# A hybrid attention, RWKV-7 and expert-retrieval layer: block-diagonal solves, a float16 choice of experts, and 24 gathered rows beside the gates

## The chip, the cores and the metric

The kernel runs on one core of a Trainium2 chip. A core has TensorE (PE: matrix products; PEld are its weight loads), VectorE (DVE), ScalarE (ACT), GpSimd (POOL) and SyncE (SP), which work side by side, and 16 DMA engines. The metric is the time of one execution on the device in microseconds (us), as the median of several runs. Times inside the execution come from one profiled execution.

## The reference

One layer over 512 latent tokens and 256 context tokens, width 1024, float32. The first half projects the normalized tokens to three branches: differential attention (8 heads), RWKV-7 heads that run in both directions (16 heads), and gates that merge the two. The recurrence of one RWKV head is

```
sa = S kk ;  S = S * w - sa (kk * a)^T + v k^T ;  y = S r
```

once in the order of the tokens and once against it. The second half is a retrieval of single-neuron experts (PEER). For every token and each of 8 heads, the 16 best of 128 row keys and the 16 best of 128 column keys are taken, then the 16 best of the 16 x 16 sums:

```
top_s, pos = lax.top_k(cand, PEER_TOPK)
eidx = jnp.take_along_axis(cidx, pos, axis=-1)
gate = jax.nn.softmax(top_s, axis=-1)
act = jax.nn.gelu(einsum('chkd,cd->chk', peer_u[eidx], xc))
out = einsum('chk,chkd->cd', gate * act, peer_v[eidx])
```

## The kernel before

The code states the work in a program order. A planner in the compiler fixes the order of every engine's instructions when the kernel is built: it simulates the program, and takes on each engine the earliest piece of work in program order that its simulation holds ready and for which a buffer is free. On the chip every engine then works through its list in that order and waits, instruction by instruction, for semaphores. A tile name in a pool has a number of buffers (bufs); a new tile of the name waits until one of them is released.

The stages, in order:

- *rw_pairs* (some 60 to 560 us): projections of the RWKV heads, eight pairs of heads. For each pair, *rw_scores* computes products of 32 tokens (a chunk), in two directions, and stores them: tD (what the triangular inverse needs), cbD and KBD. *rw_inverse* inverts the 32x32 triangles on VectorE and stores them as xD.
- The projections of the attention (560 to 740 us).
- *rwkv_chain* with the attention interleaved (742 to 1056 us for the chain). It takes 24 chunks of 32 tokens in sequence, each in two groups g of 4 pairs. Per group and chunk: *reads* (16 products against the state), a copy by ScalarE into rhs, *solve* (products with the inverted triangles XTz; here 16 of 128x32 weights by 64 columns, for two halves j and two directions), copies of the result into sv (the state's operand, 32 of its 128 rows) by ScalarE for one half and by VectorE for the other, *state* (16 products), a scaling by VectorE into the next sv, and *outputs* and *collect*. A float32 product shows as two records. The operands cb and KBt of the next chunk are loaded by SP, those of XTz and of the values (rows of sv) by POOL, each into one of two or three buffers. The unused parts of XTz and the 32 rows of sv that solve fills are zeroed by POOL once.
- The last heads of the attention, the merge of the branches and the output projection (to 1270 us).
- *peer_route* (1282 to 1558 us): the queries, and the choice of experts with top16 on VectorE for 8 heads and 4 blocks of 128 tokens. At its end the 16 chosen positions of each head are turned into keys: for each of 4 token blocks and each of the two keys (8 turns), VectorE compares 128 positions with 16 numbers (L995), multiplies with the keys (L999), and sums over the 16 (L1000).
- *peer_gates* (to 1749 us). For 384 of the tokens the experts are not gathered: all 16,384 experts are computed as dense blocks of 128, and a gate matrix picks the chosen ones. It is built in 12 chunks of 32 tokens from float16 compares and multiplies (tiles oa, obh, obl, two buffers each; L1045 to L1048), products (L1053, L1054), copies into the one stage buffer and a store of 2 MB to gD.
- *block_acts*: the product of a block of 128 experts' in-weights with the 384 tokens (ps_a; the weights split into a high and a low part by ScalarE, u_hi, L69, and VectorE, u_lo, L72). 72 of the 128 blocks come before 1757 us, as filler in routing and gates, and are parked in actD.
- The first output loop (1760 to 2243 us): for the other 56 blocks the in-product, gating, the split of the out-weights (v_hi L1132, v_lo L1133) and 18 products into ps_v per block.
- The last output loop (2243 to 2578 us): the 72 parked blocks, 18 products each, with loads of the out-weights, of the gates (gg) and of the parked activations (actl) for 8 blocks at a time.

The last 128 tokens go another way, *rows*: 128 steps gather one row of peer_u for each token by an indirect DMA of POOL (a tile gr of 128x1024 float32, 5 buffers) and take its dot product with the token (L1087), then 128 steps gather a row of peer_v and add it to the result ra (L1098). The call some(n) takes n steps of these. They start when the pool gr is opened, after the gates: 3 steps per block of the first output loop, then 2, 1, 1 in turn.

The PSUM banks: the scores of the attention (atp) have 2 buffers, its outputs 1 and, for the last 7 blocks, 3 (atr); the chain takes the rest.

## Time and profile before

| | |
|---|---|
| runs before | median 2586.62 us of 3 (2585.44 to 2592.0) |
| the profiled execution | 2591.84 us, with a span of 2590.1 us |
| busy over the span | PE 2411.5 us (93%), DVE 2025.8 (78%), ACT 1184.6 (46%), POOL 482.8 (19%) |
| mean granted TensorE clock | 0.976 of full speed |
| HBM | 470.93 MB read, 105.38 MB written, 223 GB/s over the span |
| chain that ended last | PE 62%, DVE 20%, DMA 9%, ACT 4%, issue 4% |

Busy shares are means over stages with different limits. A busy PE is not PE at its peak, since pipelined products overlap; the idle time of an engine, and what released it, says more. "Landing" of a DMA is the time from its issue to its last byte.

### The profile page before, as it was taken

What the parts mean: (1) busy time and instruction counts of PE and PEld (TensorE: products, weight loads), DVE (VectorE), ACT (ScalarE), POOL (GpSimd) and SP (SyncE); (2) the same over time, 40 slices, a digit from 0 to 9 for tenths busy, and PEclk for the clock granted to TensorE, in tenths of its full rate; (3) what the DMA queues carried; (4) which work ended last, traced back from release to release, by engine and by line L of the source; (5) the groups of instructions that cost most, each with busy time, mean ns of one, the idle gap of its engine ahead of it and who ended that gap; (6) DMA issues with size and microseconds to landing.
All of it is one profiled execution on the core that took longest, in us unless ns stands there. A gap on an engine that the chain in (4) does not pass through costs nothing.

```text
span 2590.1 us, 46535 instructions
## 1 busy us (share of the span) xinstructions
PE 2411.5 (93%) x18109; PEld 2078.5 (80%) x18109; DVE 2025.8 (78%) x3919; ACT 1184.6 (46%) x2171; POOL 482.8 (19%) x518
## 2 busy tenths in 40 slices
PE   6999999899979999899899989998999999988898
PEld 3778778798967878668688979997888998866777
DVE  5779998977748767774499998775778888788894
ACT  4666666633336666652344444552333333323332
POOL 0000000000043333000000000013444444444430
PEclk8999999999989999999899999999999999999999
DMA  5367756787487766235432536779899999899983
GB/s 226 95 164 197 185 149 167 185 264 246 136 210 209 186 175 180 81 102 166 131 109 85 176 130 232 268 284 366 313 336 336 340 339 339 324 363 372 358 327 101
DMA packets 310349, 579.75 MB, mean 224 GB/s; under 512 B 83761, under 2 KB 197041, under 8 KB 303345
## 3 DMA queue, kind: packets, MB, share of 16 engines
q1 hardware_dynamic: 253040, 387.09, 46.6%
q0 software_dynamic: 45808, 155.61, 17.5%
q10 hardware_dynamic: 11280, 34.08, 4.1%
q8 instruction: 142, 2.33, 0.4%
q14 instruction: 79, 0.64, 0.1%
HBM read 470.93 MB, written 105.38 MB: 223 GB/s over the span
## 4 chain that ended last, share of the span: by engine, by line
PE 62%; DVE 20%; DMA 9%; ACT 4%; issue 4%; SPq 0%; POOL 0%; ACTq 0%; DVEq 0%; POOLq 0%
PE ps_v L1143 6%; PE ps_v L1145 6%; PE ps_v L1142 6%; PE ps_a L80 5%; PE ps_a L78 5%; PE ps_a L79 5%; PE pp L79 3%; PE pp L80 3%; PE pp L78 3%; PE ps_s L675 2%; PE ps_br L79 2%; PE ps_br L80 2%; PE ps_br L78 2%; DMA cb<-cbD 2%; PE ps_o L808 2%
## 5 line engine op out<-in xcount | busy, mean ns | idle before, releaser
L78 PE MATMUL ps_a<-h,u_hi 128*128 128x384 f32 x1024 | 346.2, 338 | 10.0 <-ACT u_hi L69 10.0
L80 PE MATMUL ps_a<-h,u_lo 128*128 128x384 f32 x1024 | 347.2, 339 | 7.0 <-DVE u_lo L72 6.7
L79 PE MATMUL ps_a<-h,u_hi 128*128 128x384 f32 x1024 | 344.2, 336 | 0.0
L1080 POOL DMA_INDIRECT gr<-in_peer_u,ei x128 | 165.4, 1292 | 693.1 <-PE ps_a L79 472.5
L69 ACT CAST u_hi<-u_raw 128x1024 fp32r<-128x1024 f32 x128 | 134.3, 1051 | 289.8 <-PE ps_a L79 274.1
L72 DVE TENSOR_TENSOR u_lo<-u_raw,u_hi 128x1024 fp32r<-128x1024 f32 x128 | 156.3, 1221 | 102.4 <-ACT u_hi L69 101.1
L1080 POOL DMA_INDIRECT gr<-in_peer_v,ei x128 | 179.8, 1405 | 203.7 <-DVE ra L1098 182.6
L78 PEld LDWEIGHTS ps_a<-h,u_hi 128*128 128x128 f32 x1024 | 192.8, 188 | 16.1 <-ACT u_hi L69 13.7
L80 PEld LDWEIGHTS ps_a<-h,u_lo 128*128 128x128 f32 x1024 | 192.7, 188 | 12.7 <-DVE u_lo L72 11.6
L79 PEld LDWEIGHTS ps_a<-h,u_hi 128*128 128x128 f32 x1024 | 192.7, 188 | 2.4
L1098 DVE SCALAR_TENSOR_TENSOR ra<-gr,wk,ra 128x1024 f32<-128x1024 f32 x127 | 162.7, 1281 | 2.6 <-DMA gr<-in_peer_v,ei 1.5
L95 ACT CAST w_hi<-w_raw 128x1024 fp32r<-128x1024 f32 (+1 forms) x93 | 106.9, 1149 | 125.1 <-PE ps_br L79 59.3
L96 DVE TENSOR_TENSOR w_lo<-w_raw,w_hi 128x1024 fp32r<-128x1024 f32 (+1 forms) x93 | 125.0, 1344 | 49.5 <-ACT w_hi L95 43.8
L1087 DVE CUSTOM_DVE_ANT_0 gr<-gr,ht 128x1024 f32<-128x1024 f32 x128 | 153.8, 1219 | 11.2 <-DMA gr<-in_peer_u,ei 11.2
L1143 PE MATMUL ps_v<-v_lo,pw_hi 128*128 128x512 f32 x420 | 145.0, 403 | 12.0 <-DVE v_lo L1133 12.0
L1142 PE MATMUL ps_v<-v_hi,pw_hi 128*128 128x512 f32 x420 | 128.5, 400 | 16.0 <-ACT v_hi L1132 16.0
L546 PE MATMUL pp<-At,kz 128*128 128x128 f32 x768 | 106.2, 295 | 35.7 <-DVE kz L539 15.4
L78 PE MATMUL pp<-hx,w_hi 128*128 128x512 f32 x336 | 134.9, 402 | 3.4 <-ACT sgw L433 2.4
L80 PE MATMUL pp<-hx,w_lo 128*128 128x512 f32 x336 | 134.1, 399 | 2.0 <-DVE w_lo L96 2.0
L79 PE MATMUL pp<-hx,w_hi 128*128 128x512 f32 x336 | 133.0, 396 | 1.8 <-DVE hx L231 1.8
L1145 PE MATMUL ps_v<-v_hi,pw_lo 128*128 128x512 f32 x420 | 134.1, 401 | 0.0
L546 PEld LDWEIGHTS pp<-At,kz 128*128 128x128 f32 x768 | 98.4, 207 | 42.9 <-ACT kt L550 18.5
(374 smaller groups left out, 6390.7 us busy)
## 6 DMA issues: line engine op xcount, KB each, us to landing
u_raw<-in_uT SPq DMA_DIRECT2D x128, 512.0 KB, 4.6
v_raw<-in_peer_v SPq DMA_DIRECT2D x70, 512.0 KB, 8.3
w_raw<-in_peer_v SPq DMA_DIRECT2D x58, 512.0 KB, 6.5
wm<-in_w_mod SPq DMA_DIRECT2D x24, 1024.0 KB, 8.8
cb<-cbD SPq DMA_DIRECT2D x48, 512.0 KB, 6.5
gD<-gstage SPq DMA_DIRECT2D x12, 2048.0 KB, 8.3
gg<-gD SPq DMA_DIRECT2D x16, 1536.0 KB, 13.4
actD<-act SPq DMA_DIRECT2D x18, 768.0 KB, 3.6
```

The lines of the kernel that those rows point to most:

```text
L69: nc.scalar.copy(hi, raw)
L72: (lo_eng or nc.vector).tensor_tensor(lo, raw, hi.bitcast(F32), op=OP.subtract)
L78: mm(ps, lh[0], rh[0], start=first, stop=False)
L79: mm(ps, lh[0], rh[1], start=False, stop=False)
L80: mm(ps, lh[1], rh[0], start=False, stop=last)
L546: nc.tensor.matmul(ps[:, c, :], kz[:, c, :], at, start=True, stop=True)
L1080: nc.gpsimd.indirect_dma_start(out=r, out_offset=None, in_=self.A[name], in_offset=bass.IndirectOffsetOnAxis(ap=self.ei[:, k:k + 1], axis=0))
L1087: nc.vector.tensor_tensor_reduce(out=r, in0=r, in1=self.ht, scale=1.0, scalar=0.0, op0=OP.mult, op1=OP.add, accum_out=w[:, k:k + 1])
L1098: nc.vector.scalar_tensor_tensor(self.ra, r, w[:, k:k + 1], self.ra, op0=OP.mult, op1=OP.add)
L1142: mm(pc[t][d], w[0][:, ts], v[0][:, c[d]], start=first, stop=False)
L1143: mm(pc[t][d], w[0][:, ts], v[1][:, c[d]], start=False, stop=False)
L1145: mm(pc[t][d], w[1][:, ts], v[0][:, c[d]], start=False, stop=last)
```

## The change

- *Solve.* The triangles of the two halves and two directions of a pair are laid out as one 128x128 block-diagonal matrix (XTz as [128, 8, 4, 32]), so that one product of 128-column weights takes the place of four of 32-column weights. The direction 1 uses the other 32 rows of each half, so rw_scores, the mask and the zeroing swap places accordingly; tD is stored per direction (96 stores, before 48), a solve's result is one PSUM tile, and its four parts are copied to sv by two copies of ScalarE and two of VectorE, each half as large. The loads of XTz write runs of 32 elements.
- *Choice of experts.* The compare, the multiply and the sum run on float16 pairs: three halving adds and a closing add take the place of the reduction; the keys are copied to float16 pairs by ScalarE.
- *24 rows beside the gates.* After each of the 12 gate chunks two steps of rows are taken. Their tiles share the name and the two buffers of obl. The last loop takes one step per block.
- *PSUM.* The scores get 3 buffers, the last attention blocks 2.

```diff
             for j in range(2):
-                q2 = slice(64 * j + 32, 64 * j + 64)
-                nc.sync.dma_start(tD[j, cc].rearrange("c a d s t -> s (c a d) t"),
-                                  tt[q2].rearrange("p c d t -> p (c d) t"))
+                for dr in range(2):
+                    q = slice(64 * j + 32 - 32 * dr, 64 * j + 64 - 32 * dr)
+                    nc.sync.dma_start(tD[j, cc, :, dr].rearrange("c a s t -> s (c a) t"), tt[q, :, dr])
...
-        clear = lambda j, i: nc.gpsimd.memset(sv[j][i][96 - 64 * j:128 - 64 * j], 0.0)
+        vrow = lambda j, d: slice(64 - 64 * j + 32 * d, 96 - 64 * j + 32 * d)
+        urow = lambda j, d: slice(96 - 64 * j - 32 * d, 128 - 64 * j - 32 * d)
+        clear = lambda j, i: [nc.gpsimd.memset(sv[j][i][urow(j, d), d], 0.0) for d in range(2)]
         NL = 2
-        XTz = [mk(f"XTz{i}", [128, 4, 8, 32]) for i in range(NL)]
+        XTz = [mk(f"XTz{i}", [128, 8, 4, 32]) for i in range(NL)]
...
-                nc.gpsimd.dma_start(XTz[c % NL][32 * q:32 * q + 32, q], self.xD[q // 2, c, q % 2])
+                nc.gpsimd.dma_start(XTz[c % NL][32 * q:32 * q + 32, :, 3 - q], self.xD[q // 2, c, q % 2])
...
-            pu = [self.psc.tile([128, 2, 4, 64], F32, name=f"ps_u{j}") for j in range(2)]
-            for dp in range(8):
-                for j in range(2):
-                    q, ur = 2 * j + dp % 2, 96 - 64 * j
-                    nc.tensor.matmul(pu[j][ur:ur + 32, dp % 2, dp // 2, :], XTz[c % NL][:, q, 4 * g + dp // 2, :],
-                                     rhs[g][:, dp // 2, :], start=True, stop=True)
+            pu = self.psc.tile([128, 4, 64], F32, name="ps_u")
+            for a in range(4):
+                nc.tensor.matmul(pu[:, a, :], XTz[c % NL][:, 4 * g + a].rearrange("p u t -> p (u t)"), rhs[g][:, a, :],
+                                 start=True, stop=True)
             G = slice(4 * g, 4 * g + 4)
-            nc.scalar.copy(sv[0][c % NS][96:128, :, G], pu[0][96:128])
-            nc.vector.tensor_copy(sv[1][c % NS][32:64, :, G], pu[1][32:64])
+            for j in range(2):
+                nc.scalar.copy(sv[j][c % NS][urow(j, 0), 0, G], pu[urow(j, 0)])
+                nc.vector.tensor_copy(sv[j][c % NS][urow(j, 1), 1, G], pu[urow(j, 1)])
...
-                eq = wk.tile([128, 128, 16], F32, name="eq")
-                nc.vector.tensor_tensor(eq, af[:, i, :, None].to_broadcast([128, 128, 16]),
-                                        io[:, None, :].to_broadcast([128, 128, 16]), op=OP.is_equal)
...
-                nc.vector.tensor_reduce(ij[:, i, :], eq, axis=AX.X, op=OP.add)
+                sh = [128, 64, 16, 2]
+                eq = wk.tile(sh, F16, name="eq")
+                nc.vector.tensor_tensor(eq, io[:, None].to_broadcast(sh), af[:, i, :].rearrange("p (g u) -> p g u", u=2)
+                                        [:, :, None, :].to_broadcast(sh), op=OP.is_equal)
+                sd = wk.tile([128, 8, 16, 2], F16, name="sd")
+                nc.scalar.copy(sd, si[:, t, i::2, :, None].to_broadcast([128, 8, 16, 2]))
+                e4 = eq.rearrange("p (h k) a u -> p h k (a u)", h=8)
+                nc.vector.tensor_tensor(e4, e4, sd.rearrange("p h a u -> p h (a u)")[:, :, None, :]
+                                        .to_broadcast([128, 8, 8, 32]), op=OP.mult)
+                for n in (8, 4, 2):
+                    nc.vector.tensor_tensor(eq[:, :, 0:n, :], eq[:, :, 0:n, :], eq[:, :, n:2 * n, :], op=OP.add)
+                nc.vector.tensor_tensor(ij[:, i, :].rearrange("p (g u) -> p g u", u=2), eq[:, :, 0, :], eq[:, :, 1, :],
+                                        op=OP.add)
...
             nc.sync.dma_start(self.gD[ch], stg)
+            yield
...
-                self.peer_gates(b1, wk, f)
+                self.row_tile = lambda: wk.tile([128, self.TG // 2, 128, 2], F16, name="obl").rearrange(
+                    "p g k u -> p (g k u)").bitcast(F32)
+                for _ in self.peer_gates(b1, wk, f):
+                    some(2)
...
-                    some(2 if n % 3 == 0 else 1)
+                    some(1)
...
-        with self.pool("atp", 2, space=PSUM) as psS, self.pool("atq", 1, space=PSUM) as psO:
+        with self.pool("atp", 3, space=PSUM) as psS, self.pool("atq", 1, space=PSUM) as psO:
...
-                    self.pool("atr", 3, space=PSUM) as psR:
+                    self.pool("atr", 2, space=PSUM) as psR:
```

## Rows read from the trace of the kernel before

**Rows 1.** Windows: us, busy (x) PE, PEld, DVE, ACT, POOL; PEclk, DMA share, GB/s.

```profile
850.00:960.00 110.00, 100.90 (x2344) 85.67 (x2339) 73.18 (x153) 69.97 (x176) 38.46 (x77) 0.98 0.65 174
...
1520.00:1555.00 35.00, 30.06 (x159) 26.55 (x158) 35.00 (x27) 13.97 (x22) 0.00 (x0) 1.00 0.37 123
1555.00:1700.00 145.00, 144.19 (x1208) 139.54 (x1207) 121.43 (x109) 73.87 (x127) 0.00 (x0) 1.00 0.69 249
...
1780.00:2190.00 410.00, 405.33 (x2005) 363.55 (x2004) 320.04 (x456) 144.36 (x196) 171.91 (x133) 0.99 0.93 333
2190.00:2400.00 210.00, 191.74 (x830) 154.40 (x829) 173.48 (x197) 65.90 (x89) 95.42 (x67) 0.99 0.95 352
```

**Rows 2.** Groups by line, PE, 2243 to 2400 us (idle time, releaser last).

```profile
L1143 PE MATMUL ps_v<-v_lo,pw_hi 128*128 128x512 f32 x186 | 63.9, 404 | 8.2 <-DVE v_lo L1133 8.2
...
L1142 PE MATMUL ps_v<-v_hi,pw_hi 128*128 128x512 f32 x186 | 56.1, 401 | 10.0 <-ACT v_hi L1132 10.0
```

**Rows 3.** The same groups, 2400 to 2525 us.

```profile
L1143 PE MATMUL ps_v<-v_lo,pw_hi 128*128 128x512 f32 x159 | 52.2, 404 | 3.8 <-DVE v_lo L1133 3.8
...
L1142 PE MATMUL ps_v<-v_hi,pw_hi 128*128 128x512 f32 x159 | 43.8, 400 | 5.9 <-ACT v_hi L1132 5.9
```

**Rows 4.** Issues of DMAs, whole span: count, KB each, median us to landing.

```profile
gD<-gstage SPq DMA_DIRECT2D x12, 2048.0 KB, 8.3
gg<-gD SPq DMA_DIRECT2D x16, 1536.0 KB, 13.4
...
tD<-tt SPq DMA_DIRECT2D x48, 64.0 KB, 3.6
...
gr<-in_peer_u,ei POOLq DMA_INDIRECT x128, 7.7
```

**Rows 5.** Groups by line, DVE, 1480 to 1558 us.

```profile
L1000 DVE TENSOR_REDUCE ij<-eq 128x128 f32<-128x2048 f32 x8 | 18.2, 2280 | 0.0
L995 DVE TENSOR_TENSOR eq<-af,io 128x2048 f32<-128x2048 f32 x8 | 18.2, 2285 | 0.1
L999 DVE TENSOR_TENSOR eq<-eq,si 128x2048 f32<-128x2048 f32 x8 | 18.1, 2274 | 0.0
```

**Rows 6.** Groups by line, DVE, 1558 to 1700 us.

```profile
L72 DVE TENSOR_TENSOR u_lo<-u_raw,u_hi 128x1024 fp32r<-128x1024 f32 x26 | 31.7, 1221 | 20.1 <-ACT u_hi L69 20.1
L1046 DVE TENSOR_TENSOR obh<-ie,jT 128x2048 f16<-128x2048 f16 x20 | 24.4, 1224 | 3.2 <-PE ps_g L1053 3.0
```

**Rows 7.** Timeline, 918 to 921 us: start, us; one solve and its copies.

```profile
918.24 0.35 ACT L656 COPY rhs<-ps_r 128x256 f32<-128x256 f32 x1
...
919.44 1.06 PE L663 MATMUL ps_u<-rhs,XTz 128*32 128x64 f32 x32
...
920.54 0.58 ACT L666 COPY sv<-ps_u 32x512 f32<-32x512 f32 x1 [0.49 <-PE ps_u L663]
```

**Rows 8.** Costliest groups of the page: issue of a row, its dot product.

```profile
L1080 POOL DMA_INDIRECT gr<-in_peer_u,ei x128 | 165.4, 1292 | 693.1 <-PE ps_a L79 472.5
...
L1087 DVE CUSTOM_DVE_ANT_0 gr<-gr,ht 128x1024 f32<-128x1024 f32 x128 | 153.8, 1219 | 11.2 <-DMA gr<-in_peer_u,ei 11.2
```

**Rows 9.** Timeline of SP: first and last store of the gates, of 12.

```profile
1581.37 0.33 SPq L1057 DMA_DIRECT2D gD<-gstage  x1
...
1749.35 0.33 SPq L1057 DMA_DIRECT2D gD<-gstage  x1
```

**Rows 10.** Instructions of a line, ns min/median/max: weight loads, and one product.

```profile
L663 PEld LDWEIGHTS ps_u<-rhs,XTz x1536: 106/110/178, 747.5 to 1054.1; 128*32 128x32 f32 x192
L663 PE MATMUL ps_u<-rhs,XTz x1536: 216/219/316, 747.5 to 1054.1; 128*32 128x64 f32 x192
...
L808 PEld LDWEIGHTS ps_o<-va,pdT x384: 186/192/338, 790.2 to 1091.5; 128*128 128x128 f32 x192
```

**Rows 11.** DMA queues, 592 to 605 us: packets, MB, share of 16 engines.

```profile
q1 hardware_dynamic: 5684, 2.63, 73.1%
```

**Rows 12.** Chain of waits, 850 to 960 us, by line.

```profile
by line: DMA cb<-cbD 28.5%; PE ps_s L675 15.3%; PE ps_u L663 12.0%; PE ps_o L808 9.2%; PE ps_r L653 8.4%; PE ps_r L694 7.5%; PE ps_o L804 5.5%; PE ps_s L785 4.5%; PE ps_s L786 4.0%; PE ps_r L705 3.0%; issue 1.3%; ACT sv L666 0.5%; ACT yt L6
```

More of the change, by code (lines that the diff above doesn't have):

```diff
@@ L536, in rw_scores @@
                         else:
-                            eng.tensor_tensor(zo[:, :, 0, ::-1], zi[:, :, 0], w[1][h, g4], op=OP.mult)
-                            eng.tensor_tensor(zo[:, :, 1], zi[:, :, 1], w[1][h, g4], op=OP.mult)
+                            eng.tensor_tensor(zo[:, :, 1, ::-1], zi[:, :, 0], w[1][h, g4], op=OP.mult)
+                            eng.tensor_tensor(zo[:, :, 0], zi[:, :, 1], w[1][h, g4], op=OP.mult)
                     ps = self.ps.tile([128, 512], F32, name="pp").rearrange("p (c x) -> p c x", c=4)
@@ L547, in rw_scores @@
                     for j in range(2):
-                        q = slice(64 * j + 32, 64 * j + 64)
+                        q = slice(64 * j + 32 - 32 * dr, 64 * j + 64 - 32 * dr)
                         nc.scalar.copy(tt[q, c4, dr], ps[q, :, 0:32])
@@ L554, in rw_scores @@
             for j in range(2):
-                q2 = slice(64 * j + 32, 64 * j + 64)
-                nc.sync.dma_start(tD[j, cc].rearrange("c a d s t -> s (c a d) t"),
-                                  tt[q2].rearrange("p c d t -> p (c d) t"))
+                for dr in range(2):
+                    q = slice(64 * j + 32 - 32 * dr, 64 * j + 64 - 32 * dr)
+                    nc.sync.dma_start(tD[j, cc, :, dr].rearrange("c a s t -> s (c a) t"), tt[q, :, dr])
             for dst, src in ((self.cbD[:, 64:192], bt), (self.KBD, kt)):
@@ L641, in load @@
                 for d, t in enumerate((32 * c, 32 * ((7 if c < 8 else 31) - c))):
-                    nc.gpsimd.dma_start(sv[j][i][64 - 64 * j:96 - 64 * j, d], self.vTD[t:t + 32, j])
+                    nc.gpsimd.dma_start(sv[j][i][vrow(j, d), d], self.vTD[t:t + 32, j])
             for q in range(4):
-                nc.gpsimd.dma_start(XTz[c % NL][32 * q:32 * q + 32, q], self.xD[q // 2, c, q % 2])
+                nc.gpsimd.dma_start(XTz[c % NL][32 * q:32 * q + 32, :, 3 - q], self.xD[q // 2, c, q % 2])
         rhs = {}
@@ L947, in peer_route @@
         tp = b1.tile([128, 4, 8, 16], U32, name="tp")
-        io = b1.tile([128, 16], F32, name="io16")
-        nc.gpsimd.iota(io, pattern=[[1, 16]], base=0, channel_multiplier=0, allow_small_or_imprecise_dtypes=True)
+        io = b1.tile([128, 16, 2], F16, name="io16")
+        nc.gpsimd.iota(io, pattern=[[1, 16], [0, 2]], base=0, channel_multiplier=0,
+                       allow_small_or_imprecise_dtypes=True)
         def top16(vals, n, outv, outi):
@@ L989, in peer_route @@
             nc.vector.tensor_single_scalar(ab[:, 1], tp[:, t], 15, op=OP.bitwise_and)
-            af = wk.tile([128, 2, 128], F32, name="af")
+            af = wk.tile([128, 2, 128], F16, name="af")
             nc.scalar.copy(af, ab.rearrange("p i h k -> p i (h k)"))
@@ L993, in peer_route @@
             for i in range(2):
-                eq = wk.tile([128, 128, 16], F32, name="eq")
-                nc.vector.tensor_tensor(eq, af[:, i, :, None].to_broadcast([128, 128, 16]),
-                                        io[:, None, :].to_broadcast([128, 128, 16]), op=OP.is_equal)
-                e4 = eq.rearrange("p (h k) a -> p h k a", h=8)
-                sel = si[:, t, i::2, :]
-                nc.vector.tensor_tensor(e4, e4, sel[:, :, None, :].to_broadcast([128, 8, 16, 16]), op=OP.mult)
-                nc.vector.tensor_reduce(ij[:, i, :], eq, axis=AX.X, op=OP.add)
+                sh = [128, 64, 16, 2]
[11 more added lines that the diff above has]
+                                        op=OP.add)
             gt = ij[:, 2, :].rearrange("p (h k) -> p h k", h=8)
@@ L1078, in row @@
         def row(name, k):
-            r = self.gr.tile([128, D], F32, name="gr")
+            r = self.row_tile()
             nc.gpsimd.indirect_dma_start(out=r, out_offset=None, in_=self.A[name],
@@ L1176, in peer @@
                 self.pool("ga", 2, side="right") as ga, self.pool("pv", 1, space=PSUM) as pv:
+            self.row_tile = lambda: self.gr.tile([128, D], F32, name="gr")
             pc = [[pv.tile([128, 512], F32, name=f"ps_v{t}{d}") for d in range(2)] for t in range(NT)]
@@ L1419, in layout @@
     lt, le = (i[:, None] < i[None]).astype(np.float32), (i[:, None] <= i[None]).astype(np.float32)
-    A["mask"] = c(np.stack([np.tile(np.block([[a, b], [0 * lt, le]]), (2, 1))
-                            for a, b in ((lt, le), (lt[::-1], le[::-1]))], axis=1))
+    A["mask"] = c(np.stack([np.tile(np.block(m), (2, 1))
+                            for m in ([[lt, le], [0 * lt, le]], [[0 * lt, le], [lt[::-1], le[::-1]]])], axis=1))
     A["smask"] = c(np.broadcast_to((np.arange(T) % 32 != 0).astype(np.float32), (128, T)))
```

## The prediction

> **What bounds the kernel now.** I read the table by stage first. It shows three regimes that the edits touch [rows 1]. While the recurrent chain and the attention are interleaved (850 to 960 us), TensorE is busy 101 of 110 us. At the end of routing (1520 to 1555) VectorE is busy all 35 of 35 us and TensorE only 30. Through the gate stage (1555 to 1700) TensorE is busy 144 of 145 us, with the up-projections of the experts as filler, and VectorE 121. From 1780 to 2190 TensorE is busy 405 of 410 us; from 2190 to 2400 it falls to 192 of 210 while the DMA engines stand at 0.95 of their time and 352 GB/s. So the last loop is the one place where TensorE is held up by data.
>
> Second, the groups of TensorE's instructions in the last loop, with the idle time ahead of them [rows 2, 3]. The reader is to see that TensorE waits for the two halves of the value block (v_hi from ScalarE, v_lo from VectorE), 18.2 us in one window and 9.7 us in the next, 27.9 us in all, and for nothing else. Both halves start from a load that competes with the gathered rows.
>
> **The last loop.** Of the 256 gathered rows, 168 fall into the 56 blocks before this loop, today and after the change. Today 88 are left for it; with 24 done beside the gates 64 are left, one per block. A row is 128x1024 float32, 512 KB, so 24 rows are 12.6 MB: 35.7 us of DMA time at the 352 GB/s of [rows 1]. TensorE cannot win more than its idle 27.9 us. Does DMA stay the bound? A block then moves 512 KB of values, 192 KB of gates (an eighth of 1536 KB [rows 4]), 192 KB of stored activations and one row of 512 KB: 1.44 MB, 4.1 us at 352 GB/s. TensorE needs 18 products a block; 3 x 159 of them in 125 less 9.7 us [rows 3] are 0.242 us each, 4.35 us a block. So TensorE is the bound again, but by only 6%, and some waits stay. I take 24 of the 27.9 us. Bounds: -28, and -10 if the transfers still bunch. VectorE also loses 24 accumulations here, which only helps v_lo.
>
> **The choice of experts.** Today each of 8 turns does three passes over 128x2048 float32, 2.28 + 2.28 + 2.27 = 6.83 us [rows 5]. The new compare and multiply have the form of the gate stage's float16 compare over 2048, 1.22 us [rows 6]. Those two sizes give a fixed part of 0.16 us and 0.52 ns an element at the float16 rate. The three halving adds (1024, 512 and 256 elements) are then an estimated 0.69 + 0.42 + 0.29, the closing add into float32 0.29. Sum 4.13 us, 2.7 us less a turn, 21.6 us in 8. If the adds run at the float32 rate, their runs being short, it is 14 us. ScalarE gets 8 more copies of 0.35 us (the size of [rows 7]); it is busy 14 of 35 us there, so they cost nothing. VectorE is the bound of this stretch, so the gates start about 20 us earlier. But the stage ends when TensorE's list is done as well, and TensorE idles only 5 in 35 us here and 1 in 145 later [rows 1]. Of the 20 us I count at most 12 as a gain.
>
> **The 24 rows beside the gates.** 24 dot products of 1.22 us [rows 8] are 29 us for VectorE, which idles 24 us in 145 [rows 1], some 32 us over the whole gate stage: a tight fit before any wait. The wait is new. A row lives in a slot of the tile that holds the low half of the gates (two slots), so a slot now goes round like this within a chunk: multiply into it 1.22, the other multiply 1.22 [rows 6], the products (2, an estimate), issue 1.29 [rows 8], landing 7.7 [rows 4], dot 1.22: 14.7 us. VectorE and TensorE work through fixed lists, so I add two places behind another 1.22 us operation: 17.1 us. Chunks now follow every 15.3 us, (1749.35 - 1581.37)/11 [rows 9]. Behind the waiting dot stand u_lo of the filler blocks and the next chunk's compares, and TensorE waits for both. So the gates' end moves by 11 x 1.8 = +20 us, which takes back the 20 us of the earlier start. Bounds: 0 (the order hides the landing) and +52 us (20 us a chunk). With the expert choice this stage goes from -12 to +35; I take 0.
>
> **The solves.** 16 products with 32-column weights become 4 with 128-column weights (each is two records). Now 32 records take 1.06 us [rows 7], 0.84 from first to last start (a record lasts 0.22 [rows 10]). A weight load of 32 columns shows 110 ns and one of 128 columns 192 ns [rows 10]: 0.85 ns a column, so a 128-column load is an estimated 109 ns and 8 records take 0.87 us, no less than 32 narrow ones. The other bound is that the number of records counts: a quarter of 0.84, 0.63 us less, 30 us in 48 solves. I take the row of the loads and a little for the gap behind them, -5 us.
>
> [...]
>
> Against this, the copies out: two of 32x256 in place of one of 32x512 on either engine. At 0.35 us for 256 columns and 0.58 for 512 [rows 7] that is +0.12 us on the chain, +6 us in 48. The loads of the inverse matrices now land in runs of 128 bytes in place of 1 KB: 96 x 224 = 21,504 more packets. In a stretch dominated by such packets 5,684 took 73.1% of 16 engines for 13 us, 27 ns each [rows 11]; 36 us of DMA time on 16 engines, in a stage of some 315 us (742 to 1056) where the load of cb already holds 28.5% of the chain of waits [rows 12]. I take +4 us (0 to +10). The freed PSUM bank gives the scores a third buffer, -4 us (-10 to 0). Chain: -5 + 6 + 4 - 4 = +1 us, from -30 to +15.
>
> **The rest.** The scores' store tD is issued 96 times in place of 48 with the same packets; half as large, it lands no later than 3.6 us [rows 4], behind it wait only the stores of bt and kt, which have two buffers. 0 us, to +5 if that cover goes. Swapped places of the two directions, the mask and the zeroing cost nothing: same sizes. The last attention blocks have two buffers in place of three: 0 to +3.
>
> **Sum.** -24 + 0 + 1 + 0 = -23 us. The profiled execution took 2591.84 us, so 2568.8; it lies 5.2 us above the median of the runs, 2586.62, against which the forecast is 2564 us.
>
> **Rivals.**
> 1. *The chain gains too.* If records count and not columns, the solves give 20 to 30 us, with the third score buffer. For it: the chain is 12% solves [rows 12]. Against: [rows 10]. Or the landing of the rows hides and the stage keeps its 12 us. 2530 to 2555 us.
> 2. *The gain is given back beside the gates.* At some 19 us a chunk the gate stage ends 23 us later than I forecast: no change, 2579 to 2594 us. The same comes out if the last loop stays bound by DMA, at 4.1 against 4.35 us a block.
> 3. *Slower: the slot round.* One mechanism: a row's landing holds a slot of the low gate tile, VectorE stands at the dot, and the chunk waits. From 19.8 us a chunk on (2586.62 + 7.8, that is 31 us more than forecast over 11 chunks, with 17.1 as start) it decides against the change; at 21 us it gives 2564 + 43 = 2607 us. For it: only two slots, and u_lo queues behind. Against: the DMA engines stand at 0.69 of their time in that stage [rows 1], less than where most of the 7.7 us was measured.
> 4. *The float16 passes are not faster:* then the 20 us are gone and VectorE has 29 us more: 2580 us or so. Against: [rows 6].
>
> **How the numbers follow.** A run here tells no change from one of 0.3%, 7.8 us. The forecast with its own range of 2555 to 2579 has 0.46; rival 1 0.26; rivals 2 and 4 together 0.13; rival 3 0.15. Faster 0.72, same 0.13, slower 0.15. The range reaches from half-way into rival 1, 2538, to nearly the end of rival 2, 2592; it leaves out 1 in 10 on either side.
>
> **What would show it.** Right: in the last loop TensorE's idle time ahead of the products with v_hi and v_lo falls from 28 us to under 8, with the DMA share still over 0.9 in its first part; eight turns of expert choice cost VectorE some 33 us in place of 55; stores of the gates 16 to 18 us apart; 8 records of a solve in 0.9 to 1.1 us. Wrong: stores 19 us apart or more, with VectorE idle ahead of the dot product; solves of 0.5 us; a longer time to landing of cb, with TensorE idle behind it.

## The result and the profile after

The changed kernel takes 2678.73 us (median of 4 runs, 2672.85 to 2681.79) against 2588.8 us for the kernel before (4 runs): a ratio of 1.0345, 95% interval 1.0321 to 1.0369. It is slower by 89 us. The forecast was 2564 us, with a range to 2592; the rival that ends on this side, the slot round beside the gates, had 0.15. The profiled execution took 2679.8 us.

The two traces are first compared by landmarks. The last product of the chain's outputs (L705, after L709) starts at 1058.1 us before and 1091.0 after: +33. The first store of the gates: 1581.4 [rows 9] and 1594.1, so +13; the stretch between won 20 us. The last store: 1749.35 [rows 9] and 1848.9, +100; the gates lost 87. ScalarE's last cast of activations (pw_hi) in the first output loop: 2230.9 and 2324.6, +94. The end of the span: 2590.1 and 2677.9, +88; the last loop won 6. The stores of the gates on SP's timeline, first and last of 12:

```profile
1594.11 0.33 SPq L1069 DMA_DIRECT2D gD<-gstage  x1
...
1848.92 0.33 SPq L1069 DMA_DIRECT2D gD<-gstage  x1
```

They are (1848.92 - 1594.11)/11 = 23.2 us apart, before 15.3 [rows 9].

The table by stage of after, columns as in [rows 1]:

```profile
850.00:960.00 110.00, 109.16 (x1776) 89.77 (x1776) 83.77 (x202) 82.36 (x206) 41.41 (x75) 1.00 0.66 177
960.00:1060.00 100.00, 90.65 (x1677) 74.45 (x1671) 57.23 (x134) 45.88 (x119) 30.85 (x57) 0.90 0.54 149
1060.00:1095.00 35.00, 29.78 (x538) 22.80 (x538) 13.51 (x33) 8.95 (x24) 4.32 (x8) 0.74 0.39 123
1595.00:1850.00 255.00, 204.64 (x1541) 196.75 (x1540) 170.02 (x171) 94.97 (x158) 38.10 (x27) 0.90 0.68 245
...
2290.00:2500.00 210.00, 193.19 (x826) 154.93 (x825) 174.20 (x197) 65.92 (x90) 93.74 (x68) 0.98 0.95 354
2500.00:2678.00 178.00, 164.85 (x708) 130.25 (x706) 103.47 (x147) 55.38 (x74) 15.11 (x12) 0.98 0.55 192
```

The stretch of 960 to 1060 us before, which [rows 1] leaves out:

```profile
960.00:1060.00 100.00, 96.59 (x2204) 82.55 (x2204) 75.73 (x186) 63.68 (x145) 26.17 (x52) 0.98 0.57 166
```

Two things differ, and one does not. In the first stretch of the chain TensorE is fuller than before (109 of 110 us, before 101), and then emptier (91 of 100 us, before 97). Through the gates TensorE idles 50 us of 255 where it idled 1 of 145, and the granted clock is 0.90 where it was 1.00. The last loop looks as it did: 0.95 and 354 GB/s while rows come in.

**The choice of experts** went as forecast. Groups by line, VectorE, 1520 to 1600 us of after:

```profile
L1010 DVE TENSOR_TENSOR eq<-eq 128x1024 f16<-128x1024 f16 (+2 forms) x24 | 9.9, 458 | 0.0
L1002 DVE TENSOR_TENSOR eq<-io,af 128x2048 f16<-128x2048 f16 x8 | 9.6, 1220 | 0.1
L1007 DVE TENSOR_TENSOR eq<-eq,sd 128x2048 f16<-128x2048 f16 x8 | 9.6, 1218 | 0.0
...
L1011 DVE TENSOR_TENSOR ij<-eq 128x128 f32<-128x128 f16 x8 | 2.2, 284 | 0.0
```

Eight turns take 9.9 + 9.6 + 9.6 + 2.2 = 31.3 us (forecast 33) in place of 54.5 [rows 5].

**The chain.** Groups of after, 740 to 1100 us, the copies of a solve's result (idle time ahead of them, releaser last):

```profile
L671 DVE COPY sv<-ps_u 32x256 f32<-32x256 f32 x96 | 39.9, 415 | 43.5 <-ACT sv L670 42.2
...
L670 ACT COPY sv<-ps_u 32x256 f32<-32x256 f32 x96 | 34.9, 364 | 56.4 <-PE ps_u L666 49.8 <-DVE sv L671 5.2
```

VectorE stands for 42.2 us ahead of its copies, and the releaser is ScalarE's copy of the same result. The same groups before wait for the product alone:

```profile
L666 ACT COPY sv<-ps_u 32x512 f32<-32x512 f32 x48 | 27.8, 579 | 37.5 <-PE ps_u L663 37.2
...
L667 DVE COPY sv<-ps_u 32x512 f32<-32x512 f32 x48 | 32.8, 684 | 23.9 <-PE ps_u L663 22.5
```

One solve, from the timeline of after (start, us):

```profile
899.28 1.10 PE L666 MATMUL ps_u<-rhs,XTz 128*128 128x64 f32 x8
...
900.42 0.36 ACT L670 COPY sv<-ps_u 32x256 f32<-32x256 f32 x1 [0.20 <-PE ps_u L666]
...
900.81 0.94 ACT L802 ACTIVATE p<-p,rv 128x768 f32<-128x768 f32 x1
900.82 0.42 DVE L671 COPY sv<-ps_u 32x256 f32<-32x256 f32 x1 [0.20 <-ACT sv L670]
...
901.77 0.36 ACT L670 COPY sv<-ps_u 32x256 f32<-32x256 f32 x1
901.78 1.02 DVE L804 SCALAR_TENSOR_TENSOR p<-p,rv,p 128x768 f32<-128x768 f32 x1 [0.54 <-ACT p L802]
...
902.83 0.41 DVE L671 COPY sv<-ps_u 32x256 f32<-32x256 f32 x1
```

The product takes 1.10 us, as much as the 32 narrow records of [rows 7]. The four copies come in turns, ScalarE, VectorE, ScalarE, VectorE, and between two turns an attention step of 0.94 or 1.02 us slips into each engine's list: 2.86 us from the product's end to the last copy's. Before, ScalarE's single copy started 0.04 us behind the product and took 0.58 us [rows 7].

**The gates.** The way of one row, from the timelines of POOL, VectorE and TensorE of after. The first line and the last two are the other requests for rows; two go out per chunk:

```profile
1708.62 0.94 POOL L1093 DMA_INDIRECT obl<-in_peer_u,ei  x1 [13.81 <-DVE obl L1059]
1713.65 1.75 POOL L1093 DMA_INDIRECT obl<-in_peer_u,ei  x1 [4.10 <-PE ps_g L1066]
...
1724.31 1.23 DVE L1100 CUSTOM_DVE_ANT_0 obl<-obl,ht 128x1024 f32<-128x1024 f32 x1 [6.31 <-DMA obl<-in_peer_u,ei]
1725.46 1.22 DVE L1059 TENSOR_TENSOR obl<-obh,gl 128x2048 f16<-128x2048 f16 x1
...
1727.87 0.69 PE L80 MATMUL ps_a<-h,u_lo 128*128 128x384 f32 x1 [5.06 <-DVE u_lo L72]
...
1734.13 0.22 PE L1066 MATMUL ps_g<-oa,obl 128*128 128x128 f16 x1
...
1736.35 1.74 POOL L1093 DMA_INDIRECT obl<-in_peer_u,ei  x1 [20.95 <-PE ps_g L1066]
1741.06 1.74 POOL L1093 DMA_INDIRECT obl<-in_peer_u,ei  x1 [2.96 <-PE ps_g L1066]
```

The row is asked for at 1713.65 us and landed at 1724.31: 10.7 us. VectorE stood at the dot product for 6.31 of them. Behind it stood the multiply of the gates, and u_lo, for which TensorE idled 5.06 us in the middle of a filler block. That block is ahead of the gates' products in TensorE's list, so they start only at 1734.13, and the next row can be asked for at 1736.35, 22.7 us behind this one. The trace doesn't name the two slots. By chunks the round took 27 us here: two rows are asked for in each, at 1708.62 and 1713.65, then at 1736.35 and 1741.06. The mean over the stage is the 23.2 us of the stores. In groups, VectorE and TensorE of after, 1595 to 1850 us:

```profile
L1100 DVE CUSTOM_DVE_ANT_0 obl<-obl,ht 128x1024 f32<-128x1024 f32 x22 | 26.9, 1224 | 58.5 <-DMA obl<-in_peer_u,ei 58.4
```

```profile
L80 PE MATMUL ps_a<-h,u_lo 128*128 128x384 f32 x279 | 100.7, 361 | 27.3 <-DVE u_lo L72 27.3
...
L1065 PE MATMUL ps_g<-oa,obh 128*128 128x128 f16 x352 | 45.5, 226 | 15.4 <-DVE obh L1060 15.3
```

**The last loop.** Groups of TensorE, 2325 to 2680 us of after; [rows 2, 3] are parts of the same groups before, 28 us of idle time in all:

```profile
L1156 PE MATMUL ps_v<-v_lo,pw_hi 128*128 128x512 f32 x420 | 152.5, 402 | 11.4 <-DVE v_lo L1146 11.4
L1155 PE MATMUL ps_v<-v_hi,pw_hi 128*128 128x512 f32 x420 | 141.2, 400 | 10.8 <-ACT v_hi L1145 10.8
```

22.2 us are left where under 8 were forecast.

### The profile page after: what moved, and what is told of

Read it like the earlier page. It is cut to its first block, busy times and chain, and to the rows that moved or that the text cites. A ratio compares the mean times of both kernels' runs of the same rounds, so it can differ in the third digit from the quotient of the medians.

```text
span 2677.9 us, 44505 instructions
## 1 busy us (share of the span) xinstructions
PE 2459.5 (92%) x16957; PEld 2114.5 (79%) x16957; DVE 2007.9 (75%) x3991; ACT 1194.8 (45%) x2227; POOL 495.0 (18%) x524
## 3 DMA queue, kind: packets, MB, share of 16 engines
q0 software_dynamic: 45808, 155.61, 17.0%
## 5 line engine op out<-in xcount | busy, mean ns | idle before, releaser
L78 PE MATMUL ps_a<-h,u_hi 128*128 128x384 f32 x1024 | 349.8, 342 | 21.4 <-ACT acf L1128 19.5
L79 PE MATMUL ps_a<-h,u_hi 128*128 128x384 f32 x1024 | 348.6, 340 | 0.0
L69 ACT CAST u_hi<-u_raw 128x1024 fp32r<-128x1024 f32 x128 | 134.6, 1051 | 311.9 <-PE ps_a L79 295.8
L78 PEld LDWEIGHTS ps_a<-h,u_hi 128*128 128x128 f32 x1024 | 196.9, 192 | 25.3 <-ACT acf L1128 19.7
L1093 POOL DMA_INDIRECT gr<-in_peer_v,ei x128 | 172.9, 1351 | 216.3 <-DVE ra L1111 192.1
L79 PEld LDWEIGHTS ps_a<-h,u_hi 128*128 128x128 f32 x1024 | 196.3, 192 | 2.3
L1093 POOL DMA_INDIRECT gr<-in_peer_u,ei x104 | 139.7, 1343 | 178.2 <-DVE wk L1100 148.8
L1156 PE MATMUL ps_v<-v_lo,pw_hi 128*128 128x512 f32 x420 | 152.5, 402 | 11.4 <-DVE v_lo L1146 11.4
L1155 PE MATMUL ps_v<-v_hi,pw_hi 128*128 128x512 f32 x420 | 141.2, 400 | 10.8 <-ACT v_hi L1145 10.8
L1100 DVE CUSTOM_DVE_ANT_0 gr<-gr,ht 128x1024 f32<-128x1024 f32 x104 | 125.0, 1220 | 12.0 <-DMA gr<-in_peer_u,ei 11.7
L69 ACT CAST pw_hi<-actl 128x384 fp32r<-128x384 f32 x72 | 37.0, 513 | 217.0 <-PE ps_v L1156 217.0
```

Source lines behind the costliest of these rows:

```text
L69: nc.scalar.copy(hi, raw)
L78: mm(ps, lh[0], rh[0], start=first, stop=False)
L79: mm(ps, lh[0], rh[1], start=False, stop=False)
L1093: nc.gpsimd.indirect_dma_start(out=r, out_offset=None, in_=self.A[name], in_offset=bass.IndirectOffsetOnAxis(ap=self.ei[:, k:k + 1], axis=0))
L1100: nc.vector.tensor_tensor_reduce(out=r, in0=r, in1=self.ht, scale=1.0, scalar=0.0, op0=OP.mult, op1=OP.add, accum_out=w[:, k:k + 1])
L1155: mm(pc[t][d], w[0][:, ts], v[0][:, c[d]], start=first, stop=False)
```

## The experiments

Ratios are to the kernel before on the same chip; 0.001 of it is 2.6 us. Kernels that are the same up to the chain's end showed that end between 1087 and 1096 us: a landmark of one profile is good to some 5 us.

**The parts, one by one.** rows_back takes only the rows part out of the changed kernel (and the yield of the gates):

```diff
-                for _ in self.peer_gates(b1, wk, f):
-                    some(2)
+                self.peer_gates(b1, wk, f)
...
-                    some(1)
+                    some(2 if n % 3 == 0 else 1)
```

> The changed kernel with the 24 rows taken out from beside the gates again (they go back to their own buffers and to the last loop). Theory: the loss has two places, the gates with the rows (stores 23.2 us apart in place of 15.3, +87 us) and the chain (+34 us). Then stores here come 15 to 16 us apart again, the chain still ends some 34 us late, and the time is 2587 + 34 - 20 = 2601 us (2590 to 2612). Rival: the gates are slow because the late chain and the float16 choice changed the order of the filler, and the rows are not the cause: stores stay 20 us or more apart, and the time is 2650 us or more.

Measured: 2601.73 us, 1.0059 (1.0042 to 1.0077); stores 14.8 us apart (1597.30 to 1759.71); the chain ends at 1096. As the theory says.

solve_back takes out the solve, its copies, the direction swap, tD and the PSUM buffers:

```diff
-            pu = self.psc.tile([128, 4, 64], F32, name="ps_u")
+            pu = [self.psc.tile([128, 2, 4, 64], F32, name=f"ps_u{j}") for j in range(2)]
...
-        with self.pool("atp", 3, space=PSUM) as psS, self.pool("atq", 1, space=PSUM) as psO:
+        with self.pool("atp", 2, space=PSUM) as psS, self.pool("atq", 1, space=PSUM) as psO:
```

> The changed kernel with the solves, their copies, the stores of tD and the PSUM buffers as before; the float16 choice and the 24 rows beside the gates stay. Theory: the chain ends at some 1056 us again and the rest is as in the changed kernel: 2679 - 36 = 2643 us (2635 to 2652), stores of the gates some 23 us apart. Rival: the chain's lateness is hidden again later, because TensorE's filler waits for other things: 2665 us or more.

Measured: 2643.71 us, 1.0215 (1.0168 to 1.0261); the chain ends at 1060, stores are 22.9 us apart. As the theory says: the chain's lateness goes through to the end.

f16_only is the kernel before with the edits of the choice of experts alone:

```diff
-                eq = wk.tile([128, 128, 16], F32, name="eq")
+                eq = wk.tile(sh, F16, name="eq")
```

> The kernel before with the float16 choice of experts alone. Theory: the first store of the gates comes 20 to 23 us earlier, chunks stay 15 to 16 us apart, and the whole of it reaches the end: 2565 us (2560 to 2570). Rival, the forecast's own step: TensorE's list binds the stage, so that at most 12 us are left, 2575 us or more.

Measured: 2568.82 us, 0.9923 (0.9898 to 0.9948): 20 us won. The first store comes at 1554.7, 27 us earlier, and stores are 15.0 us apart. How much is left at the first output loop's start depends on the landmark: its first activation comes 10 us earlier (1751.5 against 1761.3), its first product into ps_v 29 us (1757.4 against 1786.0). At that loop's end it is 18 us. So more than the rival's 12 us is kept.

**The rows beside the gates.** rows_own4 gives them buffers of their own:

```diff
-                self.row_tile = lambda: wk.tile([128, self.TG // 2, 128, 2], F16, name="obl").rearrange(
-                    "p g k u -> p (g k u)").bitcast(F32)
+                self.row_tile = lambda: wk.tile([128, D], F32, name="rowg", bufs=4)
```

> The changed kernel with the 24 rows in four buffers of a name of their own, instead of the two of the low gate tile. Theory (slot round): the shared slots make the chunk wait for a row's landing and dot; with buffers of their own the stores come 16 to 18 us apart and the time falls by 55 to 80 us, to 2600 to 2625 us. Rival 1: the place of the dot in VectorE's list, behind a landing that is late, is what costs, whichever buffer the row has: stores stay over 21 us apart, 2660 us or more. Rival 2: half each, since four buffers let the rows be issued ahead but the dots still stand in the list: 19 to 20 us, 2635 to 2650.

Measured: 2623.58 us, 1.0141 (1.0100 to 1.0181): 53 us of the loss are gone, stores are 17.3 us apart. VectorE's group of the dots in it, 1597 to 1790 us, beside the 58.5 us of the shared slots:

```profile
L1100 DVE CUSTOM_DVE_ANT_0 rowg<-rowg,ht 128x1024 f32<-128x1024 f32 x15 | 18.1, 1219 | 7.8 <-DMA rowg<-in_peer_u,ei 7.8
```

So the shared slots are what cost 53 us. What is left against rows_back is 21 us (1.0141 less 1.0059). Two kernels take it apart.

```diff
+            r = self.row_tile() if k < 24 else row("peer_u", k)
+            nc.vector.tensor_tensor_reduce(out=r, in0=self.ht if k < 24 else r, in1=self.ht, scale=1.0, scalar=0.0,
```

> As the kernel with four buffers of their own for the 24 rows (2623.6 us), with those 24 gathers left out: the 24 dot products stay and read a tile that is resident (wrong numbers for those experts). Theory: with buffers of their own what is left, 2.5 us a chunk, is VectorE's own time, 2 x 1.22 us: stores still 17 us apart, 2616 to 2628 us. Rival: it is the landing of the rows: stores 15 to 15.6 us apart, 2592 to 2604 us.

Measured: 2620.74 us, 1.0121 (1.0085 to 1.0157): the time of the theory, but not its spacing. With no transfer to wait for, all 24 dots came at once, from 1575 to 1619 us, ahead of the first store: that came 26 us later than in rows_back (1623.4), and then the stores 15.3 us apart. The dots' time is paid without any landing.

```diff
             r = row("peer_u", k)
+            if k < 24:
+                if k == 0:
+                    nc.gpsimd.memset(w, 0.0)
+                yield
+                continue
```

> As the kernel with four buffers of their own for the 24 rows (2623.6 us), with the 24 gathers but without their 24 dot products (those experts are left out). Theory: the price beside the gates is VectorE's time, not the transfers: stores come 14.8 to 15.6 us apart, and the time is 2592 to 2604 us. Rival: the transfers of 12.6 MB slow the loads of u in this stage: stores 16 us or more apart, 2612 us or more.

Measured: 2602.53 us, 1.0065 (1.0042 to 1.0089), the time of rows_back. Stores came 16.4 us apart, a little over the theory's 15.6, but by the end of the first output loop it stood as rows_back did (last cast of pw_hi at 2254, against 2252; rows_own4 2270). So the transfers cost little there; the dot products do, wherever in this stretch they stand.

**The solve.** solve_two (on rows_back) uses the same matrix in two halves of 64 columns with a PSUM tile each, and two score buffers:

```diff
-            pu = self.psc.tile([128, 4, 64], F32, name="ps_u")
+            pu = [self.psc.tile([128, 4, 64], F32, name=f"ps_u{j}") for j in range(2)]
             for a in range(4):
+                for j in range(2):
+                    h = slice(64 - 64 * j, 128 - 64 * j)
+                    nc.tensor.matmul(pu[j][h, a, :], XTz[c % NL][:, 4 * g + a, 2 - 2 * j:4 - 2 * j].rearrange(
+                        "p u t -> p (u t)"), rhs[g][:, a, :], start=True, stop=True)
...
+            cp = [nc.scalar.copy, nc.vector.tensor_copy]
+            for d in range(2):
+                for j in range(2):
+                    cp[j](sv[j][c % NS][urow(j, d), d, G], pu[j][urow(j, d)])
```

> The changed kernel without the rows beside the gates (2601.7 us), with the block-diagonal weights used as two halves of 64 columns, whose results lie in two PSUM tiles: ScalarE copies from one, VectorE from the other; scores with 2 buffers, the last attention with 3, as before. Theory: the 34 us of the chain come from ScalarE and VectorE taking turns at the one result tile, some 0.9 us in each of 48 solves; with two tiles the waits of each engine for the other vanish, the chain ends at 1056 to 1068 us, and the time is 2568 to 2580 us. Rival: the halved copies, the runs of 128 bytes in the loads of the matrices or the two score buffers cost it, and the chain still ends after 1080 us: 2592 us or more.

Measured: 2562.01 us, 0.9897 (0.9865 to 0.9929), better than the theory; the chain ends at 1051. One solve from its timeline, and the groups of its copies, 740 to 1100 us:

```profile
918.18 0.69 PE L668 MATMUL ps_u<-rhs,XTz 128*64 128x64 f32 x16
...
918.90 0.75 ACT L674 COPY sv<-ps_u 32x256 f32<-32x256 f32 x2 [0.21 <-PE ps_u L668]
...
920.12 0.86 DVE L674 COPY sv<-ps_u 32x256 f32<-32x256 f32 x2
```

```profile
L674 DVE COPY sv<-ps_u 32x256 f32<-32x256 f32 x96 | 39.8, 415 | 18.3 <-PE ps_u L668 15.3
L674 ACT COPY sv<-ps_u 32x256 f32<-32x256 f32 x96 | 35.0, 364 | 28.4 <-PE ps_u L668 26.5
```

Neither engine waits for the other, and the product is shorter too; the score buffers differ as well. Three things could have done it; solve_one64 puts only the two tiles back into one:

```diff
-            pu = [self.psc.tile([128, 4, 64], F32, name=f"ps_u{j}") for j in range(2)]
+            pu = [self.psc.tile([128, 4, 64], F32, name="ps_u")] * 2
```

> The kernel with 64-column halves (2562.0 us), with both halves' results in one PSUM tile again; all else is the same. Theory (turns): ScalarE and VectorE copy in turns again, the waits of VectorE for ScalarE's copy come back (some 40 us in all), the chain ends 20 to 35 us later, at 1070 us or more, and the time is 2580 to 2598 us. Rival (width): the gain over the 128-column product came from the product itself, 0.69 us a solve in place of 1.10, 20 us in 48, and from two score buffers: within 6 us of 2562.

Measured: 2594.87 us, 1.0034 (1.0018 to 1.0050): 35 us lost with this one line, as the theory says. The waits are back, in the same groups:

```profile
L674 DVE COPY sv<-ps_u 32x256 f32<-32x256 f32 x96 | 39.6, 413 | 31.1 <-ACT sv L674 29.2
...
L674 ACT COPY sv<-ps_u 32x256 f32<-32x256 f32 x96 | 35.0, 365 | 47.8 <-PE ps_u L668 29.2 <-DVE sv L674 17.4
```

In this kernel each engine still copies into an sv tile of its own, as in solve_two; in the changed kernel both write into either. So the shared result tile is enough to bring the turns back.

Then the score buffers, with both widths of the product. The first kernel takes the change's three buffers, as shown; in the second the numbers are turned round:

```diff
-        with self.pool("atp", 2, space=PSUM) as psS, self.pool("atq", 1, space=PSUM) as psO:
+        with self.pool("atp", 3, space=PSUM) as psS, self.pool("atq", 1, space=PSUM) as psO:
...
-                    self.pool("atr", 3, space=PSUM) as psR:
+                    self.pool("atr", 2, space=PSUM) as psR:
```

> The kernel with 64-column halves in one PSUM tile, with 3 buffers for the scores and 2 for the last attention blocks, as in the change. The forecast's term: the third score buffer is worth 4 us, so 4 us (0 to 10) under the same kernel with two. Rival: it lets the attention run ahead into the chain's gaps, so that none of it is left for the stretch behind the chain: 0, or some us slower.

> The changed kernel without the rows beside the gates (2601.7 us), with 2 buffers for the scores and 3 for the last attention blocks, as before; the 128-column product and its one PSUM tile stay. Theory (third buffer): it lets the attention run ahead of the chain, as in the kernels with 64-column halves, where it cost 22 us; here the chain ends 12 to 25 us earlier, at 1070 to 1084 us, and the time is 2577 to 2592 us. Rival: with the 128-column product the buffers don't matter: within 6 us of 2602.

Measured: solve_one64_s3 2617.3 us, 1.0131 (1.0101 to 1.0160), 25 us slower than solve_one64, against a forecast gain of 4: the rival's side. one128_s2 2592.72 us, 1.0032 (1.0016 to 1.0049): 7 us better than rows_back, just outside the theory's range (to 2592), with intervals that just overlap. It equals solve_one64, so with one tile and two score buffers the product's width decides nothing; with three it does (rows_back is 19 us faster than solve_one64_s3), and why stays open.

What the third buffer does is seen in how much of the attention TensorE had done between 740 and 960 us (products ps_o from pdT, groups by line) beside the chain's end: 184 and 1058 us before, 192 and 1051 in solve_two, 216 and 1081 in solve_one64, 216 and 1084 in one128_s2, 228 and 1099 in solve_one64_s3, 240 and 1096 in rows_back, 240 and 1091 in the changed kernel. Broadly, the more attention went first, the later the chain ended, though the order doesn't hold between neighbours. With either width the third buffer let the lists take more of it ahead of the chain's next step; the chain's tail then has little to be mixed with (TensorE 90.65 of 100 us, 29.78 of 35 at a clock of 0.74 in the table above). That this is how the buffer costs its time is argued, not shown: a chain that is slow for another reason also leaves room for the attention, as 192 against 216 in solve_two and solve_one64 suggest.

**The last loop.** rows_paced gives the last loop's rows two buffers, on rows_own4:

```diff
+                self.row_tile = lambda: xp.tile([128, D], F32, name="grp", bufs=2)
                 held = []
```

> As the kernel with four buffers of their own for the 24 rows (2623.6 us), but in the last loop the rows have two buffers in place of five, so that they come later and more evenly: some 5 us a row in place of 3.4. Theory (bunching): TensorE's idle time ahead of the products with v_hi and v_lo, 20.9 us, comes from rows that run ahead of the blocks; it falls under 10 us and the time by 10 to 14, to 2610 to 2614 us. Rival 1: each row costs its share of idle time whenever it comes (0.33 us): no change, 2619 to 2629 us. Rival 2: two buffers are too few and the last rows come behind the blocks: over 2632 us.

Measured: 2635.66 us, 1.0188 (1.0156 to 1.0220): 12 us slower, which is the time of rival 2 but not its reason: the last addition starts at 2602.6, the blocks' last product at 2623.8. The groups of VectorE and of TensorE in its last loop, 2272 to 2636 us:

```profile
L1111 DVE SCALAR_TENSOR_TENSOR ra<-grp,wk,ra 128x1024 f32<-128x1024 f32 x64 | 82.0, 1282 | 68.4 <-DMA grp<-in_peer_v,ei 68.3
```

```profile
L1156 PE MATMUL ps_v<-v_lo,pw_hi 128*128 128x512 f32 x420 | 165.5, 411 | 25.3 <-DVE v_lo L1146 25.3
L1155 PE MATMUL ps_v<-v_hi,pw_hi 128*128 128x512 f32 x420 | 156.9, 402 | 1.3 <-ACT v_hi L1145 1.3
```

The wait for v_hi is gone (1.3 us in place of 10.8): with fewer rows on the way the value blocks come in time. But VectorE now stands 68 us at the additions, v_lo behind them, and TensorE waits 25.3 us for v_lo. So this run doesn't tell what even rows without that wait would give. Two kernels on f16_only settle what the rows cost at all.

```diff
-                    some(2 if n % 3 == 0 else 1)
                     if n == NE - 5:
-                        some(256)
```

> The kernel with the float16 choice alone (2568.8 us), with the last 88 rows left out altogether, so that its last loop has no gathers (the sums for the last 128 tokens are then incomplete). Theory: the rows' transfers are all of the idle time of TensorE there, 23.6 us; it falls to 3 us or less and the time to 2545 to 2549 us. Rival: half of it is the splitting of the value blocks and stays: 10 us or more of idle time, 2555 to 2560 us.

```diff
-            r = row("peer_v", k)
+            r = row("peer_v", k) if k < 40 else self.ht
```

> The kernel with the float16 choice alone (2568.8 us), with the last 88 rows' gathers left out and their 88 additions on VectorE kept (they read a resident tile, so the last 128 tokens get wrong sums). Theory: TensorE's idle time in the last loop comes from the transfers: under 4 us are left of 23.6, and the time is near the kernel without those rows, 2537 to 2546 us. Rival: it comes from VectorE's list, the additions standing ahead of v_lo: 10 us or more stay, 2552 us or more.

Measured: no_last_rows 2539.13 us, 0.9815 (0.9781 to 0.9849); last_nogather 2535.28 us, 0.9811 (0.9784 to 0.9838). Both lie a little below their theories' ranges. The groups of the second, 2208 to 2532 us, where VectorE still made its 88 additions:

```profile
L1151 PE MATMUL ps_v<-v_lo,pw_hi 128*128 128x512 f32 x420 | 158.7, 396 | 0.0
L1150 PE MATMUL ps_v<-v_hi,pw_hi 128*128 128x512 f32 x420 | 153.9, 397 | 0.0
```

No idle time is left in either. So the 88 gathers are all of it, and they cost 28 us of the whole (0.9923 less 0.9815), 0.32 us a row; by that 24 rows are worth 7.6 us, not 24.

two_first4, last, on solve_two, looks for a cheaper place for rows:

```diff
-                some(3)
+                some(4 if n % 2 else 3)
...
-                    some(2 if n % 3 == 0 else 1)
+                    some(1)
```

> The kernel with 64-column halves in two tiles (2562.0 us), with 28 rows moved from the last loop into the first output loop (4 and 3 a block by turns, then 1 a block). Theory: TensorE idles 5 of 410 us in the first loop, and a row of the last loop costs 0.36 us (31.5 us for 88), so that 28 of them give 8 to 10 us: 2552 to 2555 us. Rival: the first loop's transfers already fill 0.93 of the DMA time; 28 rows of 512 KB more take 40 us of it, and the first loop becomes longer by what the last one wins, or more: 2560 us or more.

Measured: 2563.5 us, 0.9916 (0.9890 to 0.9942), no gain over solve_two. But the edit moved nothing: VectorE makes 88 additions in the last loop of either kernel. So the calls in the code don't set when rows run here; that the five buffers and VectorE's list do is likely, but not shown. The rival's reason isn't shown either.

## Why the prediction was wrong, by its steps

Three terms of the forecast's -23 us failed. The rows beside the gates, together with the choice of experts, were put at 0 and came to +67 us; the chain was put at +1 and came to +33; the last loop was put at -24 and came to -6. The first output loop won 6 us, which makes the +88 us of the two traces.

**The rows beside the gates** were the largest miss: +20 us forecast, +87 measured, with the sign of being wrong that the forecast had named (stores 19 us apart or more, VectorE idle ahead of the dot). The mechanism was the forecast's own (a landing holds a slot, VectorE stands at the dot, the chunk waits), as rival 3 had it; the term of the round was mis-sized: 17.1 us, measured 23.2. Issue to landing was 10.7 us for the row shown, for 9.0. The term "two places behind another 1.22 us operation" should have been TensorE's list: from the gates' multiply to their products, forecast as 2.4 and the 2.4 for those places, it took 8.7 us (1725.46 to 1734.13), since the filler block in between itself waited for a u_lo behind the dot. TensorE was also slower behind the wait: products of the block start 0.17 us apart ahead of its 5.06 us of idle time, at a granted clock of 1.00 (1716 to 1722.8 us), 0.32 us apart behind it up to 1731.9 us, at 0.50, and 0.17 us apart again from 1732.15 on, at 1.00. rows_own4 shows the slots' share, 53 us. The forecast also set these +20 us against the full 20 us of the choice of experts, of which it had counted at most 12; by its own terms the two give +8, not 0.

That "VectorE idles 32 us over the gate stage" was taken for cover. With buffers of their own the 24 dots still cost 21 us of their 29; rows_nodot and rows_nogather put it down to VectorE's time, not to the transfers. The idle time in [rows 1] is made of waits for u_hi and for the products (20.1 and 3.0 us in [rows 6]); in rows_own4, with the dots in the list, 16.7 and 4.0 us of these waits are still there. The stretch before it, the choice of experts, has no idle time at all.

**The last loop** was to give 24 us and gave 6. Two steps failed. The count: 97 additions fell into it before, 72 after, since rows can lag behind the calls; the forecast had 88 and 64. And the threshold "one row per block, 4.1 us of DMA against 4.35 of TensorE" doesn't hold, because rows aren't spread over the blocks: the last one was asked for at 2533 us, 145 us ahead of the end, and the DMA share is 0.55 from 2500 us on. TensorE's idle time goes roughly with the rows: 28 us for 97, 22.2 for 72, 23.6 for 88 in f16_only, 20.9 for 73 in rows_own4, 0.27 to 0.31 us a row. The bound "-10 if the transfers still bunch" came nearest, and the 6 us measured are less still. That the transfers are the cause is shown (last_nogather); how much evenly spread rows would give is not, since in rows_paced VectorE's wait took the place of TensorE's.

**The chain** was to stay (+1) and lost 33 us. Of its terms:
- Solves, -5: 0. Eight 128-column records took 1.10 us; the slope of [rows 10] was right, the gap behind the loads wasn't worth anything.
- Copies, +6, priced by their length alone. The result had become one PSUM tile, which ScalarE and VectorE then had only in turns. With the same product one tile costs 35 us more than two (solve_one64 against solve_two). This was the missing step. One tile, the 128-column product and the rest of the solve together cost 28 us with two score buffers (one128_s2 against f16_only).
- Packets, +4: the count of packets of POOL's queue is 45,808 in both profiles, so the profile shows none of the 21,504 more. POOL's issue of such a load takes 584 ns for 498; no time was seen to hang on it.
- Third score buffer, -4: it cost 7 us with the 128-column product, intervals overlapping, and 25 with the halves.

**The choice of experts** held: 31.3 us for 33. Alone it gave 20 us, where "at most 12" of 20 was counted.

**tD and the rest**: nothing seen.

In sum, by ratios: choice -20 us (f16_only), solves and buffers +35 (rows_back), rows with buffers of their own +21 (rows_own4, less what the last loop gains), shared slots +53. These add up to the +89 of the change by construction, since each kernel is the one before it with a step more. solve_back checks the +35 from the other side: the change without its solve and buffers is 34 us faster.

The eight records of the changed solve are some 118 ns apart, an estimate from 1.10 us less one record of 0.275 over 7 steps, where the forecast had 109 ns a load from the slope of [rows 10]. With 1.10 us in place of 1.06 [rows 7] the fusion was worth 0 us. The copies here touch different quarters of the 128 partitions (ScalarE 96 to 127 and 32 to 63, VectorE 64 to 95 and 0 to 31), and the traces show them in turns, with 42.2 us of VectorE's waits behind ScalarE's copy. solve_one64 against solve_two shows that two tiles end that (VectorE waits 29.2 us for ScalarE's copy in the one, 15.3 us for the product in the other); whether the order is kept by tile or by bank no run here separates.

## A version that is faster than both

solve_two keeps the float16 choice and the block-diagonal matrix and drops the rest: 2562.0 us, 0.9897 of the kernel before. Against f16_only (0.9923) the solve's share is 7 us, with intervals that overlap; the float16 choice carries most of it.

## What to carry to other kernels

A result that is read by two engines belongs in two tiles: merging it into one made two parallel copies a queue (35 us here, solve_one64 against solve_two), and each turn let other work of fixed lists in between. Idle time of an engine is cover only if the operations that fill it are ready when it occurs (here the 24 dots cost 21 us of their 29); ask what it waits for there, and what stands behind the new wait on every engine, before counting it. When work is moved off a bound, price it there by the piece (here 0.3 us a row) and not by the whole idle time, and see in the trace that the code's order really sets when it runs.

## What the runs showed of the hardware that was not expected

The price of small products isn't set by the number of weight columns alone. At 1,024 columns a group it was low where neighbours go by turns to the two halves or to all four quarters of the result's 128 partitions, but not with two of the quarters: 8 records of 128 columns, all into the whole, 1.10 us; 32 of 32 columns into two quarters by turns 1.06 [rows 7]; 16 of 64 columns into the two halves by turns 0.69 (solve_two); and 32 of 32 columns into all four quarters 0.65, the reads, in the changed kernel as before:

```profile
902.98 0.65 PE L657 MATMUL ps_r<-sv,cb 128*32 128x64 f32 x32
```

That row stood in the trace of before too (L653) and would have shown it. No run here tests why.
